# Forgetting attention: one matmul for both parts of the turned probabilities, and scans without a row of resets

## The chip, the cores and the metric

The kernel runs on one core of a Trainium2 chip, as one program. The metric is device microseconds of one execution on that core. A core has five engines with a queue each, worked off in order: TensorE (PE; its weight loads are shown apart as PEld), VectorE (DVE), ScalarE (ACT), GpSimd (POOL) and SyncE (SP), which here only issues DMAs. Engines wait for each other through semaphores; a waiting instruction holds up everything behind it in its queue.

## The reference

One layer of a streaming encoder on 1024 tokens of width 1024. A combined projection feeds three mixers (a gated linear recurrence, HGRN2; forgetting attention, FoX; attention into 256 memory tokens), which are gated, summed, projected and added to the input; a ConvGLU channel mixer follows. The change touches two places. In the recurrence, the cumulative sum of log decays:

```python
f = lb + (1.0 - lb) * jax.nn.sigmoid(f_logit)
G = jnp.cumsum(heads(jnp.log(f)), axis=3)       # along the tokens of a chunk
```

and in the forgetting attention (8 heads of 64), the product of the probabilities with the values:

```python
s = (jnp.einsum('bhqd,bhkd->bhqk', qh[:, :, lo:hi], kh[:, :, :hi]) * scale
     + Fc[:, :, lo:hi, None] - Fc[:, :, None, :hi])
p = jax.nn.softmax(jnp.where(mask, s, -jnp.inf), axis=-1)
outs.append(jnp.einsum('bhqk,bhkd->bhqd', p, vh[:, :, :hi]))
```

## The kernel before, in words

All large products are done in the type fp32r in two parts. A float32 operand is split into a high part (a cast to fp32r, usually on ScalarE) and a low part (source minus high part, usually on VectorE; `split`, L134 to L136), and a product is three matmuls, high by high, low by high and high by low, that add up in one PSUM bank (`mm3`, L120 to L124). A PSUM bank has 512 float32 columns on 128 partitions.

The program runs through stages: memory keys and values; the projections of tokens by weights (with a scheme that saves one product in eight by sums of blocks); the forgetting attention; the recurrence; the branch projections; the output projection; the ConvGLU mixer. The weight units of the projections and, after them, the branch projections form one list of work, `fill`. It is woven into the attention and the recurrence: for each head, `weave` takes so many steps of attention and so many of `fill` in turn (`FOX_STEPS`, `FOX_FILL`). The attention's steps get a priority of 300 instructions ahead (`AHEAD`). From this the scheduler sets the order in each engine's queue by its own estimate of when things are ready, so an edit of a few instructions can move many others. `tc.issue_after(x)` makes an instruction wait for x.

**Forgetting attention** (`fox_attn`, L1008 to L1078), for each head h: `fox_load` (L993 to L1004) issues on SP the loads of keys (`kh`, `kl`), queries (`qa`), the row of log-forget sums (`nf`) and the values (`vhl`). For h > 0 the loads stand behind the first store of the head before (`marks["head"]`, set at L1076). `vhl` holds for each block of 128 keys the high parts of the values in 64 columns and the low parts in the next 64, so one weight load brings both, and a matmul with it gives on partitions 0 to 63 the high parts' share and on partitions 64 to 127 that of the low parts. Then come four pairs of query blocks, tp = 0 to 3, of 256 queries each. Each step of a pair:

- logits by two matmuls (L1027, L1028), bias and maximum on VectorE (L1033; the masked bias `nfm` by GpSimd, L1021), exponential on ScalarE (L1043), division by the sum on GpSimd (L1045);
- for each two blocks of keys: up to four transposes of the probabilities into a bank (`ptr`; L1056 to L1059), and the split of that bank into `ph` by ScalarE and `pl` by VectorE (L1062);
- for each block of keys two matmuls with the same weights `vhl[:, sb, :]`, one that reads `ph` and one that reads `pl` (L1068, L1069), 256 columns each. The last block of a pair concerns only 128 queries, so there both have 128 columns. All add up in the first 256 columns of the one bank `po`;
- at the pair's end ScalarE copies partitions 64 to 127 of `po` to `yp` (L1072), VectorE adds partitions 0 to 63 (L1073), and SP stores `yp` (L1074). There is one bank `po` and one tile `yp`, so the next pair's first matmul waits for L1073.

That is 8 heads x (2 + 4 + 6 + 8) blocks = 160 blocks of keys, 320 matmuls: 256 of 256 columns and 64 of 128.

**Decays of the recurrence** (`decays`, L943 to L960), once for each of 4 heads, in the midst of the attention of the first heads: SP loads a row of tanh values from DRAM (`fk`, L947), which GpSimd stored there in two halves (L776); two VectorE operations turn it into f and 1 - f (L950, L951), ScalarE takes the logarithm (L953, with a change of its tables), and VectorE makes the running sums (L956): four scans of 256 columns, which multiply the running value by a row `resets` that is 0 at the start of each 128 tokens and 1 elsewhere, and add. Four subtractions (L957) and two stores (L960) follow. `resets` is loaded once (L988).

## Time and profile before

| | |
|---|---|
| median of 3 runs | 1692.7 us (1689.22 to 1695.61) |
| profiled execution, own time | 1691.85 us |
| its span, first to last instruction | 1690.1 us |
| mean granted TensorE clock | 0.995 |
| the attention | 324 us (first loads) to 691 us (last store) |

The profile is of one execution. "Busy" is time in which an engine works on an instruction. Matmuls are pipelined: the next one begins before the last one ends, so what a matmul costs TensorE is the distance from its start to the start of the next, not its length. A wait is named by the instruction that waits and the one that released it.

### The profile page before, as it was taken

The numbers are of one execution on the slowest core, as the hardware profiler recorded it, in microseconds if no ns is written. First come the engines' busy times: TensorE is split into PE (matmuls) and PEld (weight loads), VectorE is DVE, ScalarE is ACT, GpSimd is POOL, SyncE is SP. The second block draws the span as 40 slices with busy tenths as digits, with TensorE's granted clock in tenths as the row PEclk, the third lists the DMA queues.
The fourth block names the chain that finished last, engine by engine and source line by source line (L and its number), as shares of the span: only waits on it lengthen the run. The fifth ranks groups of instructions, "written<-read, shape, count | busy, mean of one in ns | idle before, by whom it ended". The sixth has DMA issues, their size and how long they took to land.

```text
span 1690.1 us, 24934 instructions
## 1 busy us (share of the span) xinstructions
PE 1657.3 (98%) x8883; PEld 1416.6 (84%) x8883; DVE 1211.8 (72%) x2177; ACT 843.6 (50%) x1449; POOL 455.5 (27%) x482
## 2 busy tenths in 40 slices
PE   7999999999999999999999998999999999999999
PEld 5989999878788888888888787888888888888887
DVE  7875766578877666788766757877878878675664
ACT  7745554466666665556432257534434443343432
POOL 1433543556444444222102133311111111100000
PEclk9999999999999999999999999999999999999999
DMA  7352452655545542647857998766454455394772
GB/s 290 112 188 91 141 173 112 201 188 169 172 158 152 163 154 76 205 136 248 298 191 189 309 239 197 206 180 188 127 142 131 126 161 142 124 396 152 252 266 87
DMA packets 134749, 305.54 MB, mean 181 GB/s; under 512 B 14328, under 2 KB 31992, under 8 KB 133984
## 3 DMA queue, kind: packets, MB, share of 16 engines
q1 hardware_dynamic: 101008, 210.87, 36.7%
q0 software_dynamic: 24400, 78.39, 18.4%
q10 hardware_dynamic: 9216, 14.68, 2.3%
q8 instruction: 70, 1.15, 0.3%
q14 instruction: 55, 0.45, 0.1%
HBM read 223.21 MB, written 107.41 MB: 196 GB/s over the span
## 4 chain that ended last, share of the span: by engine, by line
PE 52%; DMA 2%; DVE 1%; issue 0%; ACT 0%; POOL 0%; DVEq 0%; POOLq 0%
PE pp L122 10%; PE pp L123 10%; PE pp L124 10%; PE lg L124 4%; PE lg L122 4%; PE lg L123 4%; PE tr L124 2%; PE tr L122 2%; PE tr L123 2%; DMA gt<-gd 1%; PE po L122 1%; PE po L124 1%; PE po L123 1%; PE lg L1175 1%; DMA r<-sq 0%
## 5 line engine op out<-in xcount | busy, mean ns | idle before, releaser
L1346 ACT CAST wh<-s 128x512 fp32r<-128x512 f32 x80 | 48.8, 619 | 112.5 <-PE pp L123 60.4
L128 ACT CAST dwh<-wr 128x1024 fp32r<-128x1024 f32 (+1 forms) x41 | 40.2, 980 | 114.8 <-PE tr L123 39.1
L1346 ACT CAST wh<-rw 128x512 fp32r<-128x512 f32 x70 | 43.0, 620 | 84.8 <-PE pp L123 45.5
L730 ACT CAST uh<-ur 128x512 fp32r<-128x512 f32 x78 | 48.1, 618 | 72.9 <-PE pp L123 68.4
L1470 POOL DMA_DIRECT2D rw<-in_w_up x40 | 22.3, 566 | 187.7 <-DVE wl L1347 141.8
L136 DVE TENSOR_TENSOR dwl<-wr,dwh 128x1024 fp32r<-128x1024 f32 (+1 forms) x41 | 46.3, 1130 | 36.6 <-ACT dwh L128 36.6
L731 DVE TENSOR_TENSOR ul<-us,uh 128x512 fp32r<-128x512 f32 x72 | 54.1, 757 | 24.7 <-ACT uh L730 24.5
L1045 POOL TENSOR_SCALAR pt<-pt,st 128x128 f32<-128x128 f32 (+3 forms) x64 | 56.5, 884 | 56.2 <-DVE st L1044 41.0
L1043 ACT ACTIVATE pt<-pt,st 128x128 f32<-128x128 f32 (+3 forms) x64 | 49.8, 778 | 40.5 <-DVE st L1040 34.8
L122 PE MATMUL pp<-B21h,uh 128*128 128x512 f32 x168 | 66.9, 400 | 2.4 <-DVE gt L895 2.4
L124 PE MATMUL pp<-B21h,ul 128*128 128x512 f32 x168 | 66.6, 397 | 0.0
L123 PE MATMUL pp<-T2l,uh 128*128 128x512 f32 x168 | 66.6, 396 | 0.0
L123 PE MATMUL pp<-B21l,uh 128*128 128x512 f32 x168 | 66.4, 395 | 0.0
L122 PE MATMUL pp<-T2h,uh 128*128 128x512 f32 x168 | 66.4, 398 | 0.0
L731 DVE TENSOR_TENSOR ul<-ur,uh 128x512 fp32r<-128x512 f32 x78 | 61.5, 790 | 6.4 <-ACT uh L730 5.9
L124 PE MATMUL pp<-T2h,ul 128*128 128x512 f32 x168 | 66.1, 394 | 0.0
L736 POOL TENSOR_TENSOR us<-ur 128x512 f32<-128x512 f32 x36 | 49.8, 1384 | 59.5 <-DMA ur<-in_w_cm 27.2
L730 ACT CAST uh<-us 128x512 fp32r<-128x512 f32 x72 | 43.8, 615 | 37.5 <-POOL us L736 22.1
L736 POOL TENSOR_TENSOR us<-us,ur 128x512 f32<-128x512 f32 x36 | 49.8, 1383 | 38.8 <-issue 33.2
L136 DVE TENSOR_TENSOR wl<-raw,wh 128x1024 fp32r<-128x1024 f32 x29 | 37.3, 1288 | 31.9 <-ACT wh L128 31.5
L1347 DVE TENSOR_TENSOR wl<-rw,wh 128x512 fp32r<-128x512 f32 x70 | 47.0, 686 | 17.9 <-PE pp L124 15.2
L1347 DVE TENSOR_TENSOR wl<-s,wh 128x512 fp32r<-128x512 f32 x80 | 54.7, 684 | 0.0
(721 smaller groups left out, 6159.1 us busy)
## 6 DMA issues: line engine op xcount, KB each, us to landing
rw<-in_w_up POOLq DMA_DIRECT2D x40, 512.0 KB, 4.9
ur<-in_w_cm SPq DMA_DIRECT2D x72, 256.0 KB, 3.4
sd<-in_w_dn POOLq DMA_DIRECT2D x30, 512.0 KB, 6.0
br<-yd SPq DMA_DIRECT2D x30, 512.0 KB, 4.7
gd<-uo ACTq DMA_DIRECT2D x48, 256.0 KB, 2.3
gt<-gd SPq DMA_DIRECT2D x48, 256.0 KB, 7.6
yd<-fc SPq DMA_DIRECT2D x44, 256.0 KB, 2.3
raw<-in_w_tm SPq DMA_DIRECT2D x20, 512.0 KB, 3.3
```

What stands on the lines that cost most here:

```text
L122: PE.matmul(ps, lh, rh, start=first, stop=False, skip_group_check=more)
L123: PE.matmul(ps, lh, rl, start=False, stop=False, skip_group_check=more)
L124: return PE.matmul(ps, ll, rh, start=False, stop=last, skip_group_check=more)
L128: S.copy(out, in_)
L136: return (sub or V).tensor_sub(l, src, h.bitcast(F32))
L730: marks["cast"] = S.copy(h, src)
L731: V.tensor_sub(l, src, h.bitcast(F32))
L736: G.tensor_add(t, a, b)
L1043: S.activation(pt[:, :ns], pt[:, :ns], AF.Exp, bias=st[:, 2:3], accum_out=st[:, 3:4])
L1045: G.tensor_scalar(pt[:, :ns], pt[:, :ns], st[:, 3:4], 0.0, ALU.mult, ALU.add)
L1346: late["cast"] = S.copy(h, src)
L1347: late["split"] = V.tensor_sub(l, src, h.bitcast(F32))
```

## The change

The two matmuls of a block of keys become one. `ph` and `pl` become one tile `parts` of 2 x 512 columns, and one matmul reads the same 256 columns (128 in the last block) of both halves and writes them to the two halves of the bank: the high parts' share in columns 0 to 255, that of the low parts in columns 256 to 511. There are then 160 matmuls, 128 of 512 columns and 32 of 256. The halves are added on the way out: ScalarE copies 512 columns instead of 256, VectorE adds 512 instead of 256, and a new GpSimd addition adds the halves of `yp`; SP's store waits for that one.

The scans become eight of 128 columns, each started at 0, with a constant 1 (`ones`, broadcast) as the factor. The tile `resets` and its load fall away.

```diff
-        for n in range(4):
-            sl = slice(n * 256, (n + 1) * 256)
-            V.tensor_tensor_scan(fk[:, 0, sl], resets, fk[:, 0, sl], 0.0, ALU.mult, ALU.add)
-            V.tensor_sub(fk[:, 1, sl], fk[:, 0, sl], fk[:, 1, sl])
+        for n in range(8):
+            sl = slice(n * P, (n + 1) * P)
+            V.tensor_tensor_scan(fk[:, 0, sl], ones.to_broadcast([P, P]), fk[:, 0, sl], 0.0, ALU.mult, ALU.add)
+            if n % 2:
+                sl = slice((n - 1) * P, (n + 1) * P)
+                V.tensor_sub(fk[:, 1, sl], fk[:, 0, sl], fk[:, 1, sl])
...
-    resets = pf.tile([P, 256], F32, tag="resets", name="resets")
-    SP.dma_start(resets, mats[:, 3 * P:3 * P + 256])
...
-            po = ps_po()
+            po = ps_po().rearrange("p (a c) -> p a c", a=2)
...
-                ph = pf.tile([P, HB], F32R, tag="ph", name="ph", bufs=2)
-                pl = pf.tile([P, HB], F32R, tag="pl", name="pl", bufs=2)
-                split(S, ph[:, :w], pl[:, :w], ptr[:, :w])
+                parts = pf.tile([P, 2, HB], F32R, tag="parts", name="parts", bufs=2)
+                split(S, parts[:, 0, :w], parts[:, 1, :w], ptr[:, :w])
...
-                    o = po[:, P:256] if last else po[:, 0:256]
+                    o = po[:, :, P:256] if last else po
                     src = slice(256, 384) if last else slice(jj * 256, jj * 256 + 256)
-                    PE.matmul(o, vhl[:, sb, :], ph[:, src], start=(sb == 0), stop=False)
-                    PE.matmul(o, vhl[:, sb, :], pl[:, src], start=False, stop=last)
+                    PE.matmul(o, vhl[:, sb, :], parts[:, :, src], start=(sb == 0), stop=last)
                 yield
-            yp = pf.tile([64, 256], F32, tag="yp", name="yp")
-            S.copy(yp, po[64:128, :256])
-            V.tensor_add(yp, po[0:64, :256], yp)
-            stored = SP.dma_start(yd3[1][a, p, tp * 256:(tp + 1) * 256], yp)
+            yp = pf.tile([64, 2, 256], F32, tag="yp", name="yp")
+            S.copy(yp, po[64:128, :, :])
+            V.tensor_add(yp, po[0:64, :, :], yp)
+            G.tensor_add(yp[:, 0, :], yp[:, 0, :], yp[:, 1, :])
+            stored = SP.dma_start(yd3[1][a, p, tp * 256:(tp + 1) * 256], yp[:, 0, :])
```

The order of the queues moves with it. In SP's queue, at the change from head 0 to head 1, it stands before (`hgd` is the recurrence's rows in DRAM, `ur` raw weights of the fill, `yd` the output of a mixer; numbers at names are the tile's own):

```order
L960 DMA hgd_101<-fk_4244 128x1024 x2
L783 DMA hgd_101<-uo 128x512
L1074 DMA yd_111<-yp 64x256
L997 DMA kh_4133<-kqd_93 64x1024
L998 DMA kh_4133<-kqd_93 64x1024
L997 DMA qa_4134<-kqd_93 64x1024
```

and now, in the same place:

```order
L962 DMA hgd_101<-fk_4214 128x1024 x2
L783 DMA hgd_101<-uo 128x512
L796 DMA ur<-in_w_cm 128x512
L947 DMA fk_4725<-hgd_102 128x1024
L796 DMA ur<-in_w_cm 128x512
L1073 DMA yd_111<-yp 64x256
L997 DMA kh_4105<-kqd_93 64x1024
```

Three DMAs that stood behind the loads of head 1 (two of weights, and the load of the second head's decay row `fk`, with its wait for the row's store) now stand ahead of the store and so of those loads.

In GpSimd's queue, just ahead of that store, it stands before:

```order
L1045 TENSOR_SCALAR pt<-pt,st 128x640
L775 TENSOR_SCALAR uo<-uo 128x512
L736 TENSOR_TENSOR us<-us,ur 128x512
L1021 TENSOR_TENSOR nfm<-nf,mskf 128x128
L776 DMA hgd_102<-uo 128x512
L736 TENSOR_TENSOR us<-ur 128x512
L1045 TENSOR_SCALAR pt<-pt,st 128x768
```

and now, with the new addition (L1072) among them:

```order
L775 TENSOR_SCALAR uo<-uo 128x512
L736 TENSOR_TENSOR us<-us,ur 128x512
L1045 TENSOR_SCALAR pt<-pt,st 128x640
L776 DMA hgd_102<-uo 128x512
L1021 TENSOR_TENSOR nfm<-nf,mskf 128x128
L736 TENSOR_TENSOR us<-ur 128x512
L1072 TENSOR_TENSOR yp<-yp 64x256
```

The addition comes behind the sum of weights (L736) that used to follow the same work, and the store of the decay row (L776) keeps its place behind the same three operations.

In TensorE's queue, at the second pair of head 0, it stands before:

```order
L1056 MATMUL tr<-ident,pt 128x128
L1069 MATMUL po<-pl,vhl 128x256
L1056 MATMUL tr<-ident,pt 128x128
L1068 MATMUL po<-ph,vhl 128x256
L1069 MATMUL po<-pl,vhl 128x256
L1068 MATMUL po<-ph,vhl 128x256
L1069 MATMUL po<-pl,vhl 128x256
L1068 MATMUL po<-ph,vhl 128x128
L1069 MATMUL po<-pl,vhl 128x128
```

and now:

```order
L1067 MATMUL po<-parts,vhl 128x512 x2
L123 MATMUL pp<-T1l,uh 128x512
L1027 MATMUL lg<-kh_3797,qa_3798 128x512
L1028 MATMUL lg<-kl_3799,qa_3798 128x512
L1056 MATMUL tr<-ident,pt 128x128
L1067 MATMUL po<-parts,vhl 128x512
L1067 MATMUL po<-parts,vhl 128x2x128
```

Where two matmuls of 256 columns stood one behind the other there is one of 512, and the last pair of 128 is one of 2 x 128.

## Prediction

> **What bounds the kernel now.** I began with the page's busy times, then asked for the attention's stretches (busy us of PE, PEld, DVE, ACT, POOL, then granted clock), since the change lies there alone, and then for what TensorE waits for in it.
>
> ```profile
> PE 1657.3 (98%) x8883; PEld 1416.6 (84%) x8883; DVE 1211.8 (72%) x2177; ACT 843.6 (50%) x1449; POOL 455.5 (27%) x482
> ```
>
> ```profile
> 330.00:380.00 50.00, 45.05 (x213) 36.17 (x213) 35.69 (x103) 29.97 (x51) 26.83 (x29) 0.97 0.65 209
> 430.00:480.00 50.00, 46.85 (x239) 38.96 (x238) 40.63 (x107) 31.99 (x58) 23.46 (x25) 0.97 0.54 174
> 480.00:530.00 50.00, 50.00 (x273) 42.81 (x271) 36.47 (x109) 32.16 (x68) 21.74 (x29) 1.00 0.46 144
> ```
>
> ```profile
> PE po L1068 <- DVE yp L1073: 2.4, 1, 2.4
> PE lg L1028 <- DMA kl<-kqd: 1.9, 1, 1.9
> PE lg L1027 <- DMA qa<-kqd: 1.5, 1, 1.5
> ```
>
> TensorE sets the end: it is busy 98% of the span, and all of the time between 480 and 530 us, where the attention of the later heads runs. So a shorter TensorE stream in the attention is worth its full length there. The first heads differ: between 330 and 380 it lacks 4.95 us of 50, and between 430 and 480 it lacks 3.15. There few steps of `fill` lie between attention steps, and the waits are single ones: on loads of a head's keys and on the one bank `po`. There a longer chain is felt.
>
> **The change part by part.** First the matmuls. What counts is the distance from start to start (columns: start, length):
>
> ```profile
> 460.04 0.28 PE L1068 MATMUL po<-ph,vhl 128*128 128x256 f32 x1
> 460.16 0.28 PE L1069 MATMUL po<-pl,vhl 128*128 128x256 f32 x1
> 460.28 0.28 PE L1068 MATMUL po<-ph,vhl 128*128 128x256 f32 x1
> ...
> 460.75 0.22 PE L1068 MATMUL po<-ph,vhl 128*128 128x128 f32 x1
> 460.81 0.28 PE L1069 MATMUL po<-pl,vhl 128*128 128x128 f32 x1
> 460.92 0.30 PE L1056 MATMUL tr<-ident,pt 128*128 128x128 f32 x1
> ...
> 461.29 0.39 PE L1027 MATMUL lg<-kh,qa 128*128 128x512 f32 x1
> 461.52 0.39 PE L1028 MATMUL lg<-kl,qa 128*128 128x512 f32 x1
> 461.75 0.39 PE L1027 MATMUL lg<-kh,qa 128*128 128x512 f32 x1
> 461.97 0.39 PE L1028 MATMUL lg<-kl,qa 128*128 128x512 f32 x1
> ```
>
> A matmul of 256 columns takes 0.12 us, so a block of keys takes 0.24. One of 512 takes 0.68 / 3 = 0.227. That saves 0.013 us in each of 128 blocks, 1.7 us. The last block of a pair takes 0.06 + 0.11 = 0.17 us in two matmuls of 128; one of 256 takes 0.12. That saves 0.05 us in each of 32, 1.6 us. Together **-3.3 us**. The arithmetic columns do not change; only what each instruction costs beyond them goes. The bounds are 0 (if a moving operand in two pieces cost as much as two matmuls; no row has one) and 3.3.
>
> The Trainium skill, page "TensorE: Matmul & The Clock Gate", section "Back-to-back issue gap", says that a warm isolated matmul costs its columns at 2.4 GHz and 2.5 ns; that speaks against the change, since by it (an estimate) merging saves only 2.5 ns in each of 160 blocks, 0.4 us, and the sum would come out 2.9 us higher. The trace differs: 120 ns for 256 columns, where that rule gives 109, and 110 behind the second matmul of 128, where it gives 56; so I take the rows.
>
> Next the way out and the scans. I read them from the groups (count, then busy us and mean ns):
>
> ```profile
> L1072 ACT COPY yp<-po 64x256 f32<-64x256 f32 x32 | 11.8, 369 | 17.4 <-PE po L1069 14.5 <-DMA gd<-uo 2.2
> L741 ACT COPY ue<-pp 128x512 f32<-128x512 f32 x54 | 31.4, 583 | 3.1 <-PE pp L124 3.0
> L1073 DVE TENSOR_TENSOR yp<-po,yp 64x256 f32<-64x256 f32 x32 | 13.1, 409 | 3.3 <-ACT yp L1072 3.3
> L136 DVE TENSOR_TENSOR pl<-tr,ph 128x512 fp32r<-128x512 f32 x48 | 32.1, 684 | 5.1 <-ACT ph L128 4.9
> L1021 POOL TENSOR_TENSOR nfm<-nf,mskf 128x128 f32<-128x128 f32 x64 | 34.2, 535 | 75.5 <-DVE st L1033 53.8 <-DMA nf<-negFd 9.0 <-DVE st L1040 6.0
> L736 POOL TENSOR_TENSOR us<-us,ur 128x512 f32<-128x512 f32 x36 | 49.8, 1383 | 38.8 <-issue 33.2 <-DVE ul L731 2.7 <-ACT ph L128 1.7
> L956 DVE TENSOR_TENSOR_SCAN fk<-resets,fk 128x256 f32<-128x256 f32 x16 | 12.0, 803 | 3.1 <-ACT fk L953 3.0
> ```
>
> The copy of `yp` goes from 0.369 us to that of a 512-column copy, 0.583: +0.21. The addition on VectorE goes from 0.409 to 0.684: +0.275. The GpSimd addition of 256 columns lies between 0.535 (128 columns) and 1.383 (512); a third of the way by columns gives 0.82. Over 32 pairs that is +7 us of ScalarE, +9 of VectorE and +26 of GpSimd, spread over some 330 us. VectorE at 40.6 of 50 us in its fullest stretch rises by about 1.3, and GpSimd from 23 to 27. None becomes the bound, so as sums of work they cost **0**. Scans: 32 of 128 columns for 16 of 256. I bound one by half of 0.803 and the whole of it, 13 to 26 us for 12 now, and take 13, since the rows of VectorE here grow with columns. VectorE has room; the load of `resets` is one SP issue less. Also 0. The single matmul now needs the low part too; before, the first could go ahead of it. The addition behind it hid that for one matmul only, so I take 0, with 0.68 us for any block where VectorE is late.
>
> What does cost is **latency on the store of a head's first pair**, because the next head's loads stand behind it, both in SP's queue and by `marks["head"]`. Head 0 to 1:
>
> ```profile
> 360.01 0.47 SPq L1074 DMA_DIRECT2D yd<-yp  x1
> 360.58 0.55 SPq L997 DMA_DIRECT2D kh<-kqd  x1
> ...
> 361.43 0.60 POOL L776 DMA_DIRECT2D hgd<-uo  x1
> 362.06 1.31 POOL L736 TENSOR_TENSOR us<-ur 128x512 f32<-128x512 f32 x1
> ...
> 368.71 0.22 PE L1027 MATMUL lg<-kh,qa 128*128 128x128 f32 x1
> 370.80 0.30 PE L1028 MATMUL lg<-kl,qa 128*128 128x128 f32 x1 [1.88 <-DMA kl<-kqd]
> ```
>
> ```profile
> DMA to landing us min/median/max: 2.0/2.6/6.5
> ```
>
> TensorE is already 1.88 us late here, so any delay of the loads counts in full. In the new SP queue the store has the load of `fk` ahead of it, which waits until GpSimd's store of the row (361.43, in the second row of times; its landing is the last line, for the rows in `hgd` between 340 and 420 us) has landed: 361.43 + 2.6 = 364.0. Three issues of 0.3 to 0.5 us follow (`fk`, `ur`, the store), and the loads begin at about 365.4 instead of 360.58, **+4.8 us**. GpSimd's addition is done by then (L736 ends at 363.37, + 0.82 = 364.2), so it adds nothing more. Bounds: +1.3 us if the row's store goes earlier and only the longer copy and additions (0.21 + 0.275 + 0.82) count, +8.7 if that store takes 6.5 us. I take the middle value because the loads that crowd the DMA in the old order are not yet issued in the new.
>
> Head 1 to 2, and the last change of head (6 to 7):
>
> ```profile
> 407.90 0.41 DVE L1073 TENSOR_TENSOR yp<-po,yp 64x256 f32<-64x256 f32 x1
> 408.43 0.45 SPq L1074 DMA_DIRECT2D yd<-yp  x1
> 411.02 0.92 POOL L1045 TENSOR_SCALAR pt<-pt,st 128x768 f32<-128x768 f32 x1 [4.54 <-DVE st L1044]
> 417.97 0.22 PE L1027 MATMUL lg<-kh,qa 128*128 128x128 f32 x1
> 418.29 0.30 PE L1028 MATMUL lg<-kl,qa 128*128 128x128 f32 x1
> ```
>
> ```profile
> L998 SPq DMA_DIRECT2D kl<-kqd x8: 594/596/597, 327.1 to 622.0; - x8
> ...
> DMA to landing us min/median/max: 6.0/6.3/6.9
> ```
>
> ```profile
> 628.69 0.22 PE L1027 MATMUL lg<-kh,qa 128*128 128x128 f32 x1
> 628.74 0.28 PE L1028 MATMUL lg<-kl,qa 128*128 128x128 f32 x1
> ```
>
> At head 2 the second matmul starts 0.32 us after the first, where 0.06 is usual: it just waited for its load. GpSimd is idle for 4.54 us before 411.02, so the addition starts at once, and the chain is longer by 0.275 + 0.82 = **+1.1 us**, all of it felt. At head 7 the last load is issued at 622.0 and lands 6.3 us later, at 628.3, for a use at 628.74: 0.44 us of room against 1.1, **+0.6**. For heads 3 to 6 I take 0, with 1.1 each as the upper bound.
>
> The bank `po` comes free 0.5 us later (0.21 + 0.275). That is felt only where the next pair follows closely, as in the 2.4 us wait of the list; 0 to +1 us, taken as 0, because four scans in a row held VectorE there and the new order may part them.
>
> Sum: -3.3 + 4.8 + 1.1 + 0.6 = +3.2 us. On the profiled execution's own 1691.85 us that is **1695 us**. That execution lies 0.85 us under the median of the runs shown, far less than the spread between the runs, so I don't correct for it.
>
> **The rivals.**
> - *Only the matmuls count.* The loads' delay is covered, because new order puts other work ahead of the head's first logits, or the row's store lands early. For it: between 480 and 530 us TensorE waits for nothing. Against: 1.88 us of waiting at head 1 today. Time 1691.85 - 3.3 = 1688.6.
> - *The first heads' holes close.* The new order happens to part scans and `yp`, and loads come in time: up to the 4.95 + 3.15 us that TensorE lacks there, and the matmuls: 1691.85 - 3.3 - 8.1 = 1680.5. For it: the holes are single waits. Against: every chain that ends in them gets longer.
> - *Every change of head waits (slower).* The place is SP's queue: the store now waits for GpSimd, which works off sums of weights of 1.38 us (L736) and divisions ahead of the addition, and the loads behind it wait as well. It decides from about 0.4 us of delay at head 7, and from nothing at heads 1 and 2. With two such sums (2.8 us) and the 1.1 ahead of all seven stores, 3.9 us less some 0.5 of room at five heads is 17, at head 2 3.9, at head 1 up to 8.7: bounded by 1691.85 - 3.3 + 30 = 1718; half of it, since GpSimd idles half of the time, gives 1704.
> - *VectorE and GpSimd get late.* Both rise by some 10% in the first heads, where a cast or a logit that comes later stops TensorE: half a microsecond at each of 20 steps of the first two heads on top of the sum's -3.3 + 1.1 + 0.6 is 1691.85 + 8.4 = 1700.
>
> **How the numbers follow.** About 0.5% (8.5 us, so below 1683.4 or above 1700.3) is what a measurement of this kernel can tell from no change. Chances: the forecast 0.46, only the matmuls 0.25, holes close 0.06, every change of head 0.15, late engines 0.08. The first two lie within 0.5%; the third is faster; of the fourth I put 0.13 above the bound and of the last 0.03. That makes 0.06 faster, 0.78 within, 0.16 slower. The range reaches down to the matmuls alone with 2 us for the order, 1686, and up to the fourth case's 1704, which leaves out the third, half of the fourth and a little of the second.
>
> **What the profile after would show.** Right: L1067 as 128 matmuls of 512 columns some 0.227 us apart and 32 of 256; PE waiting longer than 1.9 us for `kl` or `qa` at head 1, its loads issued some 5 us later after the first pair; the GpSimd addition at about 0.8 us; no wait for loads beyond 1 us at heads 3 to 7. Wrong: a distance of 0.24 us behind the 512-column matmuls; loads of head 1 that start as early as now; waits on `yp` or casts that together exceed those on loads.

## The result and the profile after

The change makes the kernel slower: 1712.92 us in the median of 5 runs (1708.38 to 1713.37) against 1692.7 us (5 runs, 1689.22 to 1695.61), a ratio of 1.012 (95% interval 1.0108 to 1.0133). The forecast was 1695 us with a range from 1686 to 1704. The profiled execution took 1713.11 us, 21 us more than the one of before.

The page's busy times of the changed kernel:

```profile
PE 1663.4 (97%) x8723; PEld 1410.7 (82%) x8723; DVE 1223.8 (72%) x2193; ACT 848.7 (50%) x1449; POOL 483.6 (28%) x514
```

TensorE has 160 instructions less and is busy 6 us longer, in a span 21 us longer: it does not have more work, it waits more and for part of the time runs at half clock. First the matmuls themselves (start, length; groups of two):

```profile
456.83 0.62 PE L1067 MATMUL po<-parts,vhl 128*128 128x512 f32 x2
457.29 0.27 PE L1056 MATMUL tr<-ident,pt 128*128 128x128 f32 x1
...
458.08 0.51 PE L1067 MATMUL po<-parts,vhl 128*128 128x512 f32 x2
458.44 0.39 PE L122 MATMUL pp<-T1h,uh 128*128 128x512 f32 x1
```

Two of 512 columns take 0.46 us; one of 512 and one of 2 x 128 take 0.36. Over all records the median distance is 232 ns behind a matmul of 512 and 119 behind one of 256; before it was 119 for 256 columns, and 59.5 and 113 for the two of 128. That is 128 x 0.006 + 32 x 0.0535 = 2.5 us saved. The saving is there.

The way out, in groups (count, busy us, mean ns, idle time before them), and the scans:

```profile
L1072 POOL TENSOR_TENSOR yp<-yp 64x256 f32<-64x256 f32 x32 | 27.3, 852 | 18.0 <-DVE yp L1071 17.6
L1071 DVE TENSOR_TENSOR yp<-po,yp 64x512 f32<-64x512 f32 x32 | 21.7, 678 | 6.4 <-ACT yp L1070 6.1
L1070 ACT COPY yp<-po 64x512 f32<-64x512 f32 x32 | 18.7, 584 | 12.6 <-PE po L1067 9.7 <-PE tr L1059 2.3
L956 DVE TENSOR_TENSOR_SCAN fk<-ones,fk 128x128 f32<-128x128 f32 x32 | 14.0, 500 | 3.1 <-ACT fk L953 3.1
```

These are the durations that were forecast (0.82, 0.684 and 0.583 us; 13 us of scans). The first change of head, with SP's, GpSimd's and TensorE's rows:

```profile
366.40 0.60 POOL L776 DMA_DIRECT2D hgd<-uo  x1
...
369.62 0.73 POOL L1072 TENSOR_TENSOR yp<-yp 64x256 f32<-64x256 f32 x1
```

```profile
369.13 0.32 SPq L947 DMA_DIRECT2D fk<-hgd  x1
...
370.37 0.48 SPq L1073 DMA_DIRECT2D yd<-yp  x1
370.94 0.55 SPq L997 DMA_DIRECT2D kh<-kqd  x1
```

```profile
378.32 0.48 PE L1027 MATMUL lg<-kh,qa 128*128 128x128 f32 x2 [2.42 <-DMA qa<-kqd]
380.46 0.47 PE L1028 MATMUL lg<-kl,qa 128*128 128x128 f32 x2 [1.66 <-DMA kl<-kqd]
```

The load of `fk` waits for the row's store (366.40 + 2.7 us), the store of `yp` and the loads follow it. So this place behaves as the forecast had it, but TensorE's waits there grow by 2.2 us (2.42 + 1.66 instead of 1.88), not by 4.8.

Most of the time is lost elsewhere. To see where, I cut TensorE's stream at five points and took from each stretch 0.2267 us for every fill matmul (L122 to L124) in it, the distance from start to start on which the forecast rested. What is left, "net", can be compared though the order moves fill from one stretch to another. (28.0 - 120 x 0.2267 = 0.8, in the fourth row.)

| stretch | before: us, fill, net | after: us, fill, net | difference of net |
|---|---|---|---|
| up to the first logits | 331.6, 2124 | 338.4, 2124 | +6.8 us (same instructions) |
| attention, up to the first product of the recurrence | 373.2, 1116, 120.2 | 398.7, 1202, 126.2 | +6.0 |
| recurrence | 206.1, 636, 62.0 | 206.0, 640, 60.9 | -1.1 |
| from it to the output projection | 28.0, 120, 0.8 | 18.5, 54, 6.3 | +5.5 |
| output projection | 118.5, 468, 12.4 | 117.1, 444, 16.4 | +4.0 |
| the rest | 628.8 | 629.3 | +0.5 |

The attention got 25.5 us longer, but 19.5 of these are 86 fill matmuls that the new order draws into it; 6.0 us are lost, although the matmuls save 2.5. The 86 matmuls are then missing behind the recurrence: 66 fewer there and 24 fewer in the output projection, where 9.5 us are lost (8.4 with the recurrence itself). And the first 6.8 us lie ahead of the first changed instruction. The granted clock (last but two columns) differs there, most of all in two stretches, here before:

```profile
12.20:19.00 6.80, 6.43 (x26) 4.71 (x27) 4.23 (x7) 6.01 (x13) 0.00 (x0) 1.00 1.04 417
39.50:46.30 6.80, 6.80 (x41) 5.97 (x40) 4.32 (x6) 3.41 (x6) 4.41 (x1) 1.00 0.69 231
```

and here after:

```profile
12.20:19.00 6.80, 6.28 (x16) 4.78 (x16) 4.60 (x7) 6.40 (x11) 0.00 (x0) 0.50 1.04 417
39.50:46.30 6.80, 5.80 (x16) 4.24 (x15) 6.11 (x8) 3.50 (x6) 6.67 (x1) 0.50 0.49 161
```

At half the clock far fewer matmuls start, with the same instructions. A third such stretch runs from 114.6 to 118.0 us; in the three together (17.0 us) TensorE was busy for 15.5, so half of that, 7.7 us, is an estimate of what they cost. A second profile of the same kernel (e9, below) doesn't have this delay. In the attention and behind the recurrence the clock explains nothing: its mean is 0.99 in the attention and 0.98 from the end of the recurrence to that of the output projection, before and after alike.

Head by head, the attention loses its time in head 2: net 17.7 us before, 23.6 after (+5.9); the other seven heads together have -0.6, and what lies between their last product with the values and the recurrence +0.7. Its stretch before (busy us of PE, PEld, DVE, ACT, POOL, then clock):

```profile
418.00:468.80 50.80, 48.31 (x248) 40.77 (x247) 40.43 (x109) 34.89 (x60) 23.70 (x25) 0.97 0.63 200
```

and after:

```profile
430.10:488.40 58.30, 51.09 (x234) 39.94 (x234) 46.95 (x121) 35.01 (x59) 33.88 (x32) 0.97 0.52 165
```

TensorE lacks 7.2 us there instead of 2.5 (before, that was the one wait of 2.4 us for `yp` in the prediction's list). It now waits for (us, times, longest):

```profile
PE pp L124 <- DVE ul L731: 2.4, 1, 2.4
PE lg L1027 <- DVE st L1033: 2.0, 1, 2.0
PE lg L1028 <- DMA kl<-kqd: 1.2, 1, 1.2
PE pp L122 <- DVE ue L148: 1.1, 1, 1.1
```

Three of four are VectorE, and two of these concern the fill's own operands (`ul`, `ue`). These operands stand in VectorE's queue behind the work of the decays. Its scans run there in blocks:

```profile
439.95 4.05 DVE L956 TENSOR_TENSOR_SCAN fk<-ones,fk 128x128 f32<-128x128 f32 x6 [0.74 <-ACT fk L953]
469.01 2.63 DVE L956 TENSOR_TENSOR_SCAN fk<-ones,fk 128x128 f32<-128x128 f32 x8 [0.46 <-ACT fk L953]
```

The `ul` for which TensorE waits 2.4 us comes at 445.83, behind the first block, and the `ue` at 474.82, behind the second. VectorE also stands still in this head with all that behind it (in brackets the idle time and who ended it); the operation on the logits (L1033), for which TensorE waits 2.0 us, comes at 465.15, right behind the last of these rows:

```profile
435.25 0.81 DVE L950 TENSOR_SCALAR fk<-fk,nc,c1p 128x1024 f32<-128x1024 f32 x1 [2.12 <-DMA fk<-hgd]
457.90 0.29 DVE L1033 CUSTOM_DVE_ANT_0 pt<-lg,nfm 128x128 f32<-128x128 f32 x1 [2.26 <-POOL nfm L1021]
464.42 0.81 DVE L950 TENSOR_SCALAR fk<-fk,nc,c1p 128x1024 f32<-128x1024 f32 x1 [2.88 <-DMA hgd<-uo]
```

In the kernel before, head 2 has for such work 1.69 and 0.66 us:

```profile
426.38 0.82 DVE L950 TENSOR_SCALAR fk<-fk,nc,c1p 128x1024 f32<-128x1024 f32 x1 [1.69 <-DMA fk<-hgd]
454.12 0.81 DVE L950 TENSOR_SCALAR fk<-fk,nc,c1p 128x1024 f32<-128x1024 f32 x1 [0.66 <-issue]
```

Behind the recurrence, the two stretches up to the end of the output projection before:

```profile
911.00:939.00 28.00, 28.00 (x128) 22.92 (x127) 20.18 (x30) 10.22 (x16) 8.17 (x10) 1.00 0.94 257
939.00:1057.50 118.50, 111.39 (x485) 91.10 (x483) 78.73 (x102) 67.12 (x99) 34.89 (x40) 0.97 0.97 242
```

and after:

```profile
943.10:961.60 18.50, 15.65 (x61) 11.83 (x60) 13.82 (x22) 8.85 (x15) 5.69 (x8) 0.91 0.89 272
961.60:1078.70 117.10, 104.77 (x461) 85.27 (x459) 70.97 (x92) 62.57 (x94) 37.52 (x42) 0.99 0.98 241
```

TensorE lacks 0 + 7.1 us before and 2.9 + 12.3 after. Its longest waits in both stretches together, after:

```profile
PE lg L122 <- DVE x L1395: 3.5, 2, 2.5
PE po L1406 <- DMA r<-sq: 3.0, 1, 3.0
PE pp L122 <- DVE x L1395: 2.9, 1, 2.9
PE pp L122 <- DVE gt L895: 2.4, 2, 1.8
PE pp L122 <- ACT T2h L128: 1.5, 1, 1.5
```

and before:

```profile
PE pp L122 <- DVE gt L895: 2.4, 1, 2.4
PE po L1407 <- DMA r<-sq: 2.2, 1, 2.2
PE pp L122 <- DVE r L1324: 1.6, 1, 1.6
```

Those on `x` and on `T2h` are new.

The chain that seems to need cover there, read from the times of these rows and not tested, is after: accumulating DMAs on GpSimd's queue (L921, then L1275), by which an operand `T1h` of the output projection is made; ScalarE waits for it, and VectorE for ScalarE.

```profile
976.86 1.05 ACT L128 CAST B11h<-T1h 128x1024 fp32r<-128x1024 f32 x1 [11.44 <-DMA T1h<-T1l]
977.95 1.23 DVE L136 TENSOR_TENSOR B11l<-T1h,B11h 128x1024 fp32r<-128x1024 f32 x1 [7.90 <-ACT B11h L128]
```

ScalarE's wait for the same operand took 1.34 us before:

```profile
961.99 1.05 ACT L128 CAST B11h<-T1h 128x1024 fp32r<-128x1024 f32 x1 [1.34 <-DMA T1h<-T1l]
```

### The profile page after: what moved, and what is told of

It is laid out like the page before. It is cut to its first block, busy times and chain, and to the rows that moved or that the text cites. A ratio compares the mean times of both kernels' runs of the same rounds, so it can differ in the third digit from the quotient of the medians.

```text
span 1711.3 us, 24662 instructions
## 1 busy us (share of the span) xinstructions
PE 1663.4 (97%) x8723; PEld 1410.7 (82%) x8723; DVE 1223.8 (72%) x2193; ACT 848.7 (50%) x1449; POOL 483.6 (28%) x514
## 5 line engine op out<-in xcount | busy, mean ns | idle before, releaser
L1345 ACT CAST wh<-s 128x512 fp32r<-128x512 f32 x80 | 48.8, 619 | 113.0 <-PE pp L123 60.9
L122 PE MATMUL pp<-B21h,uh 128*128 128x512 f32 x168 | 66.8, 400 | 2.4 <-DVE gt L895 2.4
L122 PE MATMUL pp<-T2h,uh 128*128 128x512 f32 x168 | 66.1, 397 | 1.9 <-ACT T2h L128 1.5
L124 PE MATMUL pp<-T2h,ul 128*128 128x512 f32 x168 | 67.2, 401 | 0.0
L124 PE MATMUL pp<-B21h,ul 128*128 128x512 f32 x168 | 66.3, 394 | 0.0
L736 POOL TENSOR_TENSOR us<-ur 128x512 f32<-128x512 f32 x36 | 48.6, 1350 | 62.4 <-DMA ur<-in_w_cm 31.4
L1021 POOL TENSOR_TENSOR nfm<-nf,mskf 128x128 f32<-128x128 f32 x64 | 37.6, 588 | 88.8 <-DVE st L1033 63.9
L1045 POOL TENSOR_SCALAR pt<-pt,st 128x128 f32<-128x128 f32 (+3 forms) x64 | 52.6, 823 | 33.9 <-DVE st L1044 26.5
L136 DVE TENSOR_TENSOR parts<-tr,parts 128x512 fp32r<-128x512 f32 (+1 forms) x80 | 50.0, 629 | 7.8 <-ACT parts L128 7.6
```

Of the source, the lines that this page charges most:

```text
L122: PE.matmul(ps, lh, rh, start=first, stop=False, skip_group_check=more)
L124: return PE.matmul(ps, ll, rh, start=False, stop=last, skip_group_check=more)
L136: return (sub or V).tensor_sub(l, src, h.bitcast(F32))
L736: G.tensor_add(t, a, b)
L1045: G.tensor_scalar(pt[:, :ns], pt[:, :ns], st[:, 3:4], 0.0, ALU.mult, ALU.add)
L1345: late["cast"] = S.copy(h, src)
```

## The experiments

Eighteen more runs were made, each of them beside the kernel before on the same chip; the ratio compares with that, and the kernel before has medians from 1691.03 to 1692.79 us there. The terms are read from one execution of each, so a term is good to some 3 us (the run with the scans alone differs by 3.0 us behind the recurrence with the same number of fill matmuls), and in some kernels (e7, e17, e18) the profiled execution was 5 us faster than the median. "Left" counts the fill matmuls between the recurrence and the output projection; "attention" and "behind" are differences of net to the kernel before (behind: recurrence to the end of the output projection). The fill of the attention is counted up to the first product of the recurrence; the recorded expectations count it only up to the attention's last product with the values (1053 before, 1139 after).

| run | median us | ratio, 95% interval | attention: fill, net | left, behind |
|---|---|---|---|---|
| before | 1692.7 | | 1116 | 120 |
| after | 1712.92 | 1.012 (1.0108 to 1.0133) | 1202, +6.0 | 54, +8.4 |
| e1 scans only | 1693.98 | 1.0015 (0.9999 to 1.0032) | 1116, +0.1 | 120, +3.0 |
| e2 way out only | 1700.71 | 1.0054 (1.0036 to 1.0072) | 1164, +7.2 | 119, -1.7 |
| e3 halves on VectorE | 1721.54 | 1.016 (1.0123 to 1.0197) | 1224, +19.0 | 54, +13.4 |
| e4 two `yp` | 1692.54 | 1.0001 (0.9987 to 1.0014) | 1116, +2.2 | 120, -0.4 |
| e5 one more step | 1698.74 | 1.0041 (1.0027 to 1.0055) | 1116, +8.1 | 120, -0.9 |
| e6 merge only | 1709.26 | 1.0109 (1.0084 to 1.0134) | 1176, +5.5 | 79, +10.7 |
| e7 less in attention | 1705.54 | 1.0077 (1.0049 to 1.0106) | 1164, +8.2 | 119, +0.3 |
| e8 before, more woven in | 1699.82 | 1.0051 (1.0033 to 1.0069) | 1142, +2.1 | 101, +4.7 |
| e9 after again | 1708.45 | 1.0111 (1.0095 to 1.0127) | 1202, +6.7 | 54, +8.9 |
| e10 after, no logarithm | 1708.94 | 1.0115 (1.01 to 1.013) | 1202, +9.0 | 54, +9.6 |
| e11 before, no logarithm | 1691.26 | 0.9998 (0.9985 to 1.001) | 1116, +2.1 | 120, -0.5 |
| e12 before, 500 ahead | 1696.63 | 1.0043 (1.0028 to 1.0059) | 1116, +0.2 | 104, +4.0 |
| e13 after, rows ready | 1701.73 | 1.0064 (1.0041 to 1.0087) | 1202, -1.9 | 54, +12.0 |
| e14 after, other weave | 1704.79 | 1.0076 (1.0061 to 1.0091) | 1164, +11.8 | 119, +1.5 |
| e15 merge, three steps | 1703.27 | 1.0067 (1.0052 to 1.0083) | 1190, +4.3 | 79, +8.4 |
| e16 after, rows early | 1707.71 | 1.0099 (1.0073 to 1.0125) | 1200, +5.2 | 54, +9.4 |
| e17 three steps, rows early | 1700.61 | 1.0044 (1.0031 to 1.0057) | 1200, -2.1 | 101, +6.9 |
| e18 before, rows early | 1702.99 | 1.006 (1.0042 to 1.0078) | 1164, +5.7 | 119, +1.0 |

### Taking the change apart: e1 to e4

I began with the theory that the longer way out stretches the attention (A), against the scans (B), the clock of one execution (C) and the merged matmul (D).

**e1**, the kernel before with the new scans:

```diff
-        for n in range(4):
-            sl = slice(n * 256, (n + 1) * 256)
-            V.tensor_tensor_scan(fk[:, 0, sl], resets, fk[:, 0, sl], 0.0, ALU.mult, ALU.add)
...
+        for n in range(8):
+            sl = slice(n * P, (n + 1) * P)
+            V.tensor_tensor_scan(fk[:, 0, sl], ones.to_broadcast([P, P]), fk[:, 0, sl], 0.0, ALU.mult, ALU.add)
...
```

> The kernel before with the change's scans alone: eight scans of 128 columns instead of four of 256 and no row of resets; two matmuls and the old way out stay. Theory A (the longer way out of each pair stretches the chain of the attention, TensorE fills the holes with work that is then missing behind the recurrence): the scans don't touch that, 1689 to 1696 us, the attention (first product of queries and keys to last product with v) within 2 us of the 358.3 us of the kernel before, 1053 fill matmuls in it. Theory B (the scans are the cost): 1705 to 1713 us. Theory C (the 6.8 us by which the changed kernel is late before any changed instruction belongs to that run's clock and not to the change): the first product of queries and keys is at 331 to 334 us in this run; if such a delay comes and goes from run to run it may stand at 338 us here too.

1693.98 us, no difference that can be told. B falls.

**e2**, the changed kernel with two matmuls again, from `ph` and `pl` as tiles of their own:

```diff
...
-                    PE.matmul(o, vhl[:, sb, :], parts[:, :, src], start=(sb == 0), stop=last)
+                    PE.matmul(o[:, 0, :], vhl[:, sb, :], ph[:, src], start=(sb == 0), stop=False, skip_group_check=True)
+                    PE.matmul(o[:, 1, :], vhl[:, sb, :], pl[:, src], start=False, stop=last, skip_group_check=True)
```

> The changed kernel with its matmul taken apart again: two matmuls of 256 columns, the high part into the first half of the bank and the low part into the second, with the new way out and the new scans. Theory A (the way out is the cost): as slow as the changed kernel or slower by up to the 4.3 us that the merged matmul saves there, 1709 to 1718 us, with the attention 380 us or longer. Theory D (the merged matmul is the cost, since it waits for both parts and takes the bank longer in one piece): back at 1692 to 1697 us, the attention at 360 us. Theory C (clock of one run): the first product of queries and keys between 331 and 334 us.

1700.71 us, between the two: the way out (with the new scans) costs 8 us, all of it in the attention, and the merged matmul, which saves 2.5 us where it stands, brings another 8 to 12 (by the changed kernel's two medians, 1708.45 and 1712.92 us). Neither A nor D as they were put. The first logits stand at 332.3 us, as C has it.

**e3**, the halves added on VectorE:

```diff
-            G.tensor_add(yp[:, 0, :], yp[:, 0, :], yp[:, 1, :])
+            V.tensor_add(yp[:, 0, :], yp[:, 0, :], yp[:, 1, :])
```

> The changed kernel with the addition of the two halves on VectorE instead of GpSimd: 0.41 us instead of 0.73 us, and no crossing to another engine. Theory A in the form that the latency of each pair's way out is the cost: the crossing to GpSimd and its waits (17.6 us in 18 waits) go, so the time falls by a third to a half of the 20 us, 1702 to 1707 us. Theory A in the form that the amount of fill drawn into the attention is the cost: the order of this kernel has 1163 fill matmuls there (1139 in the changed kernel, 1053 before), so 1713 to 1720 us, with the attention 385 us or longer. Theory D (the merged matmul): unchanged, 1711 to 1714 us.

1721.54 us, still slower and above every forecast, though the step that adds the halves got shorter (0.41 us in the median instead of 0.73). So a shorter step there doesn't bring the loss down. But this order also draws the most fill of all into the attention (1224), so the run doesn't show that the chain costs nothing.

**e4**, e1 with a second `yp`:

```diff
-            yp = pf.tile([64, 256], F32, tag="yp", name="yp")
+            yp = pf.tile([64, 256], F32, tag="yp", name="yp", bufs=2)
```

> The kernel before with the change's scans and a second buffer for the sum on the way out, so that a pair's copy out of the bank doesn't wait for the store of the pair before. Theory A (the chain of a pair's way out sets the attention's length): if the single buffer is part of that chain, the attention gets shorter than 358.3 us and the kernel 1 to 4 us faster than before, 1688 to 1692 us. Rival (the buffer is free in time, since the store takes about 2 us and a pair over 10 us): the time of the run with the scans alone, within 2 us.

1692.54 us: the single buffer costs nothing that can be measured.

### One suspected cost at a time: e5 to e8

The theory was now split: the chain of each pair (A1), or the fill that the order draws forward and that is then missing (A2).

**e5**, before (with the new scans) and one more step on GpSimd:

```diff
+            G.tensor_scalar(yp, yp, 1.0, 0.0, ALU.mult, ALU.add)
             stored = SP.dma_start(yd3[1][a, p, tp * 256:(tp + 1) * 256], yp)
```

> The kernel before with the change's scans and one more operation on GpSimd (times 1, plus 0, on the 64 x 256 tile of sums) between VectorE's addition and the store: the change's crossing to GpSimd without its matmul, its longer copy and its longer addition. The order leaves the fill in the attention at 1053 matmuls, as before. Theory A1 (every pair's longer chain adds to the attention): 32 pairs x 0.73 us, so up to 23 us, at least 1705 us. Theory A2 (what costs is the fill that another order draws into the attention, not the chain itself): only the loads of the next head begin later, by some 0.7 to 1.5 us at the 7 changes of head, of which the first two count: 1693 to 1698 us.

1698.74 us. Not the 23 us of A1; 7 us, in the attention, none behind. Heads 0 and 2 have them (+4.3 and +5.3); the five heads from 3 on have +0.5 together. Most of it is waiting for the loads of the next head, 7.8 us where the kernel before has 1.9:

```profile
PE lg L1028 <- DMA kl<-kqd: 5.0, 3, 2.8
PE lg L1027 <- DMA qa<-kqd: 2.8, 1, 2.8
```

That is the mechanism of the forecast, by itself.

**e6**, the merged matmul with the old way out, of the first half alone:

```diff
-            yp = pf.tile([64, 2, 256], F32, tag="yp", name="yp")
-            S.copy(yp, po[64:128, :, :])
-            V.tensor_add(yp, po[0:64, :, :], yp)
-            G.tensor_add(yp[:, 0, :], yp[:, 0, :], yp[:, 1, :])
...
+            yp = pf.tile([64, 256], F32, tag="yp", name="yp")
+            S.copy(yp, po[64:128, 0, :])
+            V.tensor_add(yp, po[0:64, 0, :], yp)
...
```

> The changed kernel with the old way out, of the first half of the bank alone: a copy of 256 columns, one addition of 256, the store; the low parts' share in the second half is left out of the result. It is the merged matmul by itself. Its order has 1113 fill matmuls in the attention and 79 between the recurrence and the output projection (changed kernel 1139 and 54, before 1053 and 120). Theory A1 (the way out is the cost): 1686 to 1692 us. Theory A2 (the fill drawn into the attention is then missing behind the recurrence): between before and the changed kernel, 1698 to 1707 us, with waits of 3 us or more between the recurrence and the output projection, which the kernel before doesn't have.

1709.26 us, above the forecast, with no operation in it that takes longer. What this kernel loses comes through the order, but for the single matmul's wait for the low part, 1.1 us in the attention. Its largest wait from the recurrence to the end of the output projection, 9.3 us in five pieces:

```profile
PE pp L122 <- DVE gt L895: 9.3, 5, 3.3
```

**e7**, the changed kernel in another weave:

```diff
-FOX_STEPS, HGRN_STEPS = 28, 14
-FOX_FILL = [2, 6, 5, 5, 5, 5, 5, 5]
+FOX_STEPS, HGRN_STEPS = 20, 14
+FOX_FILL = [2, 6, 4, 4, 4, 4, 4, 4]
```

> The changed kernel with other numbers for the weaving: 20 steps of attention to 2, 6, 4, 4, 4, 4, 4, 4 of fill, instead of 28 to 2, 6, 5, 5, 5, 5, 5, 5. All of the change stays. The order then has 1092 fill matmuls in the attention (1139) and 119 between the recurrence and the output projection (54), nearly the distribution of the run with the new way out and two matmuls (1089 and 119). Theory A2 (the fill's place is what the change costs most of): the time of that run less what the merged matmul saves there, 1695 to 1701 us, with no waits behind the recurrence. Theory A1 or D (the way out or the matmul itself): as the changed kernel, 1709 to 1714 us.

1705.54 us, between the two forecasts; its profile took 1700.86. Behind the recurrence the loss is gone (+0.3); the attention loses as much as before.

```profile
PE po L1406 <- DMA r<-sq: 3.0, 1, 3.0
PE pp L122 <- DVE gt L895: 2.2, 1, 2.2
```

In this list of the same stretches, of which these are the two longest, the changed kernel's 3.5, 2.9 and 1.5 us on `x` and `T2h` are missing.

**e8**, the kernel before in another weave:

```diff
-FOX_FILL = [2, 6, 5, 5, 5, 5, 5, 5]
+FOX_FILL = [2, 6, 6, 6, 5, 5, 5, 5]
```

> The kernel before, nothing of the change, with two more steps of fill woven into the attention (2, 6, 6, 6, 5, 5, 5, 5 instead of 2, 6, 5, 5, 5, 5, 5, 5). Its order has 1092 fill matmuls in the attention (1053) and 101 between the recurrence and the output projection (120). A control: theory A2 expects that the order alone, without any longer operation, costs some us, 1695 to 1703 us. Theory A1 or D: nothing, 1690 to 1694 us.

1699.82 us: two numbers of the weave cost 8 us, with every operation as it was. The profile has +2.1 us in the attention and +4.7 behind.

### The two terms: e9 to e12

**e9** is the changed kernel once more, with no edit.

> The changed kernel once more, unchanged. In its first profile the attention began 6.8 us later than in the kernel before, though no instruction ahead of it differs; the profiles of eight other kernels with the same instructions there began between 1.5 us earlier and 1.8 us later. If that delay belongs to the one execution, the first product of queries and keys stands at 330 to 334 us here, and the time is 1706 to 1713 us; if it belongs to the kernel, at 337 to 340 us. The attention again 380 to 386 us, the waits behind the recurrence again 5 us or more.

1708.45 us; the first logits are at 330.5 us, 1.1 ahead of the kernel before. So the 6.8 us belonged to the one execution; whether the other executions of that session, with a median of 1712.92 us, had such a delay too isn't known, since only one was profiled. Both terms come out as in the first profile: +6.7 and +8.9 us.

**e10** and **e11**, after and before without the changes of ScalarE's tables:

```diff
-            S.activation(fk, fk, AF.Ln)
+            S.activation(fk, fk, AF.Copy, scale=-0.1)
```

> The changed kernel with the logarithm of the decays replaced by a copy times -0.1 (so the decays are not those of the reference). The order of every engine stays the same, only the two changes of ScalarE's tables at each of the four heads' decays are gone, 2 x 1.28 us of a hold of 4.5 us. Theory A3 (what is lost in the attention is lost at these holds: ScalarE, and VectorE behind it with the scans, are late for the fill that TensorE has next, and the changed order puts the third of them where TensorE has nothing else): the first four heads get 4 to 8 us shorter, and the time falls to 1703 to 1709 us, by more than in the kernel before with the same edit. Rival (the holds are covered, the loss is spread over the pairs): 1711 to 1714 us.

> The kernel before with the same edit: the logarithm replaced by a copy times -0.1, the order of every engine the same, two changes of tables less at each of four heads. Theory A3: the kernel before has its holds at places where TensorE has work, so it gains less than the changed kernel, 0 to 3 us: 1689 to 1693 us. Rival: the same gain in both, whatever it is.

1708.94 and 1691.26 us: no gain in either. A3 falls.

**e12**, the kernel before with 500 ahead:

```diff
-AHEAD = 300
+AHEAD = 500
```

> The kernel before, nothing of the change, with the attention and the recurrence set 500 instead of 300 instructions ahead. Its order keeps 1053 fill matmuls in the attention, but has 676 in the recurrence (636) and 104 between it and the output projection (120). A control for the second term alone. Theory A2 (fill that was used up earlier is missing behind the recurrence, where a chain of DMAs and of the last head's sums has to be covered): 3 to 6 us slower than before, 1694 to 1699 us, all of it behind the first product of the recurrence. Rival (the waits behind the recurrence of the changed kernel have another cause): 1690 to 1694 us.

1696.63 us. The attention is unchanged (+0.2), and +4.0 us lie behind the recurrence, with 16 fewer fill matmuls left. The term exists without the change. The output projection's stretch:

```profile
942.60:1060.00 117.40, 106.75 (x460) 86.23 (x459) 74.09 (x95) 66.31 (x98) 35.56 (x40) 0.97 0.97 245
```

TensorE lacks 10.7 us in it, where it lacked 7.1.

### Head 2, and the terms as a forecast: e13 to e18

**e13**, e10 with the decay rows loaded from an input that is there from the start:

```diff
-        SP.dma_start(fk[:, 0, :], hgd[h][0])
+        SP.dma_start(fk[:, 0, :], x_rows[h])
```

> The changed kernel with the copy in place of the logarithm and the decay rows loaded from an input that is there from the start instead of from the row that the projections have just stored (so the decays are not those of the reference). The order keeps 1139 fill matmuls in the attention and 54 behind the recurrence. In the run without the logarithm VectorE sat 9.3 us idle ahead of its work on the stored rows (3.7 for their loads, 2.9 and 2.7 for the store ahead of a load and of another row), with all of the attention's and the fill's low parts queued behind. Theory A4 (that idling is what heads 0 to 3 lose): head 2 is 4 us or more shorter, the time 1700 to 1705 us, and the waits behind the recurrence stay. Rival (the loss comes from the order in all engines, with no single cause): 1707 to 1711 us.

1701.73 us, 7 less than e10. Head 2's loss is gone (net -0.9 us against +8.2 in e10), the loss behind the recurrence stays. VectorE's only standstill for such a row in head 2:

```profile
437.01 1.02 DVE L950 TENSOR_SCALAR fk<-fk,nc,c1p 128x1024 f32<-128x1024 f32 x1 [3.46 <-DMA fk<-in_x_rows]
```

VectorE still stood 8.2 us for these loads in all, but 4.7 of them in heads 0 and 1. The run doesn't part two effects: the load of `fk` in SP's queue no longer holds up the loads of the next head either. From e10 to e13 TensorE's waits for loads fall from 6.2 to 3.4 us, those for VectorE from 7.7 to 3.7.

**e14**, the changed kernel in another weave:

```diff
-FOX_STEPS, HGRN_STEPS = 28, 14
-FOX_FILL = [2, 6, 5, 5, 5, 5, 5, 5]
+FOX_STEPS, HGRN_STEPS = 20, 14
+FOX_FILL = [2, 4, 4, 5, 5, 5, 5, 6]
```

> The changed kernel, all of it, with 20 steps of attention to 2, 4, 4, 5, 5, 5, 5, 6 of fill. Its order has 1090 fill matmuls in the attention, 74 between it and the recurrence, 589 in the recurrence and 119 behind it. Theory A2, used as a forecast: with 119 left there is no loss behind the recurrence (within 2 us of before), the attention loses 5 to 9 us net of its fill, so 1697 to 1703 us. Rival (the two terms were read into the runs afterwards): anywhere from 1690 to 1713 us, and the waits behind the recurrence don't follow the count.

1704.79 us, just above the forecast's 1697 to 1703. The half of the forecast on what lies behind the recurrence held (+1.5), the half on the attention did not (+11.8 instead of 5 to 9).

**e15**, the merged matmul with a way out of three steps of 256 columns:

```diff
-            yp = pf.tile([64, 2, 256], F32, tag="yp", name="yp")
-            S.copy(yp, po[64:128, :, :])
-            V.tensor_add(yp, po[0:64, :, :], yp)
-            G.tensor_add(yp[:, 0, :], yp[:, 0, :], yp[:, 1, :])
+            yp = pf.tile([64, 256], F32, tag="yp", name="yp")
+            S.copy(yp, po[64:128, 0, :])
+            V.tensor_add(yp, po[0:64, 0, :], yp)
+            V.tensor_add(yp, po[0:64, 1, :], yp)
...
```

> The merged matmul with another way out, all on 256 columns and without GpSimd: ScalarE copies the low parts' share of the first half, VectorE adds the high parts' share of the first half and then that of the second; the product of low part by low part (the fourth quarter of the bank) is left out of the sum. One buffer of 256 columns. Its order has 1128 fill matmuls in the attention and 79 behind the recurrence. Theory A2, used as a forecast: 8 to 11 us lost behind the recurrence, 4 to 8 us in the attention, so 1703 to 1711 us, though its chain is only 0.4 us longer than before. Theory A1 (the way out is the cost): 1690 to 1697 us.

1703.27 us, with +4.3 and +8.4: inside the forecast at its lower edge, both terms as expected.

**e16**, the changed kernel with the decay rows projected first:

```diff
-UNITS = [[("f", 0), ("q", 0)], [("g", 0), ("f", 1)], [("q", 1), ("g", 1)], [("f", 2), ("q", 2)],
-         [("g", 2), ("f", 3)], [("q", 3), ("g", 3)]]
+UNITS = [[("f", 0), ("f", 1)], [("q", 0), ("f", 2)], [("g", 0), ("f", 3)], [("q", 1), ("g", 1)],
+         [("q", 2), ("g", 2)], [("q", 3), ("g", 3)]]
```

> The changed kernel, all of it, with the units of fill in another order: the projections of the decay rows of all four heads come first (f0 with f1, then q0 with f2, g0 with f3, and the rest), so that the rows of heads 2 and 3 lie in DRAM well before they are loaded. Its order has 1128 fill matmuls in the attention, 72 behind it, 642 in the recurrence, 54 behind the recurrence. Theory A4 (in the changed kernel the place of the decays' work, late in head 2 behind the stores of its rows, is what heads 0 to 3 lose): head 2 within 2 us of before net of its fill, the loss behind the recurrence stays at 8 to 10 us: 1698 to 1704 us. Rival (no single cause): head 2 again 4 to 8 us, 1706 to 1713 us.

1707.71 us, the rival's time, but with head 2 as A4 has it: it is cured (+0.6). Heads 0 and 1 now lose 3.8, and with the end of the attention the sum is +5.2. TensorE's longest wait in head 1 is for a split that VectorE did late:

```profile
PE tr L1056 <- DVE parts L136: 3.9, 1, 3.9
```

**e17**, e15 with the rows projected first as in e16 and 24 steps to 2, 6, 4, 4, 4, 4, 4, 4 of fill.

> The merged matmul with the way out in three steps on 256 columns (low by low left out), the decay rows projected first, and 24 steps of attention to 2, 6, 4, 4, 4, 4, 4, 4 of fill. Its order has 1140 fill matmuls in the attention and 101 behind the recurrence. If both terms are understood: 4 us lost behind the recurrence as in the other runs with 101 to 104, nothing or up to 3 us gained in the attention: 1691 to 1698 us. If not: 1700 us or more.

1700.61 us, above its range, though its profile (1695.82 us) shows the attention 2.1 us shorter net than before; behind the recurrence it loses 6.9 us instead of 4. It is the fastest merged kernel and still slower than before.

**e18**, the kernel before with rows projected first:

```diff
-UNITS = [[("f", 0), ("q", 0)], [("g", 0), ("f", 1)], [("q", 1), ("g", 1)], [("f", 2), ("q", 2)],
+UNITS = [[("f", 0), ("f", 1)], [("g", 0), ("f", 2)], [("q", 1), ("g", 1)], [("q", 0), ("q", 2)],
```

> The kernel before, nothing of the change, with the decay rows of heads 0 to 2 projected first (f0 with f1, g0 with f2, q1 with g1, q0 with q2, g2 with f3, q3 with g3). Its order has 1102 fill matmuls in the attention and 119 behind the recurrence. A control: if early rows take waits out of the heads' beginning in general, 1687 to 1692 us; if they only mend what the changed order broke, as before or a little slower, 1691 to 1697 us, with no loss behind the recurrence.

1702.99 us: slower than either forecast, with no loss behind the recurrence (+1.0). Early rows are no gain in themselves.

## Why the prediction was wrong

- *TensorE sets the end, and its stream in the attention counts in full*: held. But "the change lies there alone" is the step that failed first. The instructions of the change do; its effect doesn't. More than half of what is lost behind the first logits, 8.4 of 14.9 and 8.9 of 16.3 us net in the two profiles, lies behind the recurrence, 220 us further on. The sum has no term for it.
- *Matmuls -3.3 us*: right in kind, 2.5 by the medians. The saving on 512 columns was half of what I took (0.006 us a block instead of 0.013), that on the 2 x 128 right (0.0535 instead of 0.05). By the rule of the Trainium skill that the prediction weighed (page "TensorE: Matmul & The Clock Gate", section "Back-to-back issue gap": for an isolated matmul the columns at 2.4 GHz and 2.5 ns) it would have been 0.4 us, an estimate; the rows, with 172.5 ns behind two matmuls of 128 against 119 behind one of 256, still speak against it.
- *Way out and scans 0 as sums of work*: the durations were right, and none of these engines became a bound. What I drew from it was wrong. An order that follows from estimated times answers to every duration and every merged instruction. Of the changed kernel's parts, the scans alone move no fill and cost nothing (e1); with them, the way out costs 8 us (e2) and the matmul 18 (e6), and the last has no operation that takes longer. I had read the moved order at three places for their own sake and not counted what it did to the fill: 86 matmuls, 19.5 us, used up early. The single matmul's wait for the low part, also taken as 0, was one of 1.2 us (1.7 in e9).
- *Store and loads at head 0 to 1, +4.8 us*: the mechanism was right, down to the load of `fk` that waits 2.7 us for the row, and the size too large. Counted from the first logits the loads begin 3.5 us later, and TensorE's waits there are 2.42 + 1.66 us instead of 1.88, so +2.2. Other waits got shorter: heads 0 and 1 together lose -0.1 and +2.0 us net in the two profiles. *Head 1 to 2, +1.1*: one wait for `kl` of 1.2 us instead of 0.3. *Head 7, +0.6*: no loss; heads 5 to 7 have -1.2 net.
- *The bank free later, 0*, since "the new order may part" the scans from it: the wait for `yp` is gone, but in head 2 others took its place, +5.9 and +5.1 us. The new order didn't part the scans there: six and eight stand in a row, and the fill's operands now wait behind them. I had priced a place of trouble as likely to get better as worse.
- *The rivals*: the slower ones each kept the order as it is and made an engine or a queue late. The late engines came nearest in the attention, but as three waits for VectorE in head 2 (5.5 us instead of 2.4), not as half a microsecond at each of 20 steps. None had the fill in it.
- *The signs*: the longer waits for `qa` and `kl` at head 1, the 0.85 us of GpSimd's addition, no wait for loads above 1 us at heads 3 to 7 all came as the prediction set them for being right. They could not tell, since all of them look at the attention's own operations and none behind it.

What is shown: the order alone, without any of the changed operations, costs 6 to 10 us (1696.63, 1699.82 and 1702.99 us in e12, e8 and e18, against 1691.03, 1691.66 and 1692.79 of the kernel before beside them), and the term behind the recurrence follows the fill that is left there. With 119 or 120 matmuls left it lies between -1.7 and +3.0 us in eight profiles, with 101 to 104 between 4.0 and 6.9 in three, with 54 to 79 between 8.4 and 13.4 in eight. That the missing cover is the cause, and not something else that these orders share, is the reading that fits; it was not isolated. Every order with fewer than 119 left also has 24 fewer fill matmuls inside the output projection, and the changed kernel's own attention with 120 left behind the recurrence was not run.

The term of the attention is understood in part. It arises with the way out, with the matmul, and with one more step. By TensorE's waits behind the first logits, those for loads of a head are 5.8 and 5.2 us in the two profiles instead of 1.9, those for VectorE 7.9 and 8.9 instead of 3.9: the first is the prediction's own mechanism, the second lies for the most part at the decays' work of head 2. With one more step (e5) it is the loads alone, 7.8 us against 2.3 for VectorE. The term goes when the decays' rows come from elsewhere (e13), and moves from head 2 to heads 0 and 1 when the rows are made earlier (e16).

What stays open is its size for a given order. VectorE's standstill for the rows does not measure it: e5 has 1.1 us of it in head 2 and loses 5.3 there, e14 has 3.6 and loses 7.8. And e14's miss shows that I can't forecast it from an order.

## What to carry to other kernels

Where a scheduler fills one stage's holes from a common stock of work, cost an edit by what it does to that stock, in instructions counted in the order of both kernels, and look at the stage that gets the rest, however far away. A duration that no engine feels can still move the order, so an edit that saves 3 us on the bound engine is worth trying only with a few other weaves beside it. Run neutral edits (numbers of the weave, the order of the units) first: here three of them cost 6, 8 and 10 us (e12, e8, e18), so a loss of that size says little about an edit's own work. No order tried here was faster than that of the kernel before.

## What the runs showed of the hardware

- The same instructions took 331.6 us in one execution and 338.4 in another. The first had a granted clock of 1.00 up to there, the second 0.50 in three stretches of 6.8, 6.8 and 3.4 us. Sixteen other profiles with the same work of TensorE ahead of the attention reach its first logits between 329.9 and 333.3 us. Ahead of the first of these stretches, TensorE's rows in the first profile of the changed kernel:

```profile
11.60 0.74 PE L122 MATMUL pp<-wh,T4h 128*128 128x512 f32 x2 [1.80 <-ACT wh L128]
12.86 0.79 PE L123 MATMUL pp<-wl,T4h 128*128 128x512 f32 x1 [0.52 <-DVE wl L136]
```

  In its second, e9, the same two waits took 1.33 and 0.52 us, and the clock fell there too, but for one stretch of 3.4 us:

```profile
12.70:16.10 3.40, 3.40 (x10) 2.63 (x9) 2.30 (x5) 3.10 (x7) 0.00 (x0) 0.50 1.03 416
```

  The Trainium skill (page "TensorE: Matmul & The Clock Gate", section "What's actually happening") says that the clock is halved after an idle window of some 3.4 us; in both executions less idle time, in two pieces, went ahead of it.
- The addition of 64 x 256 elements on GpSimd took 0.852 us in the mean and 0.73 in the median; a scan of 128 columns 0.399 us in the median and up to 1.451.
- One matmul over two pieces of 256 columns costs 232 ns from start to start, little less than two of 256 (238 ns), while one over two pieces of 128 costs 119 against 172.5: the gain lies in the short ones.
